# Weight loads moved to ScalarE's queue, gates ahead of transposes and queries, and a third buffer for the window tables of a one-core hybrid block

## The chip, the cores and the metric

The kernel runs on one core of a Trainium2 chip. The time is the device time of one execution in microseconds (us). The engines are PE (TensorE, matmuls), DVE (VectorE), ACT (ScalarE), POOL (GpSimd) and SP (SyncE, which only starts transfers). A DMA is started by an instruction on the queue of an engine (here of SP, ACT or POOL), and every engine works through its instructions strictly in the order that was fixed when the program was built.

## The reference, cut to what matters

Two layers over 512 latent and 256 context tokens, width 1024. Layer 0 is multi-head latent attention with 16 heads, layer 1 a bidirectional S5 state-space layer with a GLU; the weights are modulated by `c`.

```python
for i in range(DEPTH):                       # 0: attention, 1: S5
    sh, sc, gt = jnp.split(cond @ w_mod[i] + b_mod[i], 3, axis=-1)
    h_lat = x * (1.0 + sc[:, None]) + sh[:, None]
    y_lat, y_ctx = _mla_mixer(...) if kind == 0 else _s5_mixer(...)
    x = _layernorm(DEEPNORM_ALPHA * x + gt[:, None] * y_lat, ln_g[i], ln_b[i])
# layer 0
q_dn, kv_dn, k_rope, gate = jnp.split(h @ w_in, MLA_SPLITS, axis=-1)   # gate: 16 heads x 128
q_abs = jnp.einsum('bnhd,chd->bnhc', q[..., :MLA_NOPE], w_uk)
p = jax.nn.softmax(s_all * scale)            # 768 keys
v = jnp.einsum('bnhc,chv->bnhv', o_lat, w_uv); y = (v * silu(gate)) @ w_out
# layer 1: per group of 16 channels, 64 complex states
lam_bar = jnp.exp(lam * dt); powers = jnp.exp(lam_dt * arange(1, 129))
xs = scan of lam_bar * x + b_bar @ u; y = real(xs @ cmat)
```

## The kernel before, in words

Every product in full precision is three matmuls of split operands: `split` writes a high part on ACT (a cast, L65) and a low part `source - high` on DVE or, where it is asked for, on POOL (also L65). A projection is then `mm<-hh,whi`, `mm<-hl,whi`, `mm<-hh,wlo` (L81 to L83).

A scheduler fixes each engine's order at build time from the order of the code and its own estimate, so an edit moves instructions far from its own line. All transfers that SP's and ACT's queues start share eight semaphores in turn, so an issue can also have to wait for the transfer that had its semaphore before.

The stages, by the profile's times:

- 0 to 72 us: the input, the first modulation (L574), and the first projections of layer 0 (queries, keys, rotary part).
- 72 to 349 us, the **gate stage**: 16 gates, one for each head (`gate(m)`), each 48 matmuls, a tanh on ACT (L698) and a multiply on DVE (L699). The products of layer 1's and layer 0's remaining modulation run between them (`mod_steps`; a *step* is one 768 KB load of `w_mod` into a tile `pair`, L98, and the matmuls `modps<-pair` of L103). In the same stage POOL computes the parameters of S5 (`s5_params`: complex products `cmul`, L237 to L242, on 128x128 tiles that lie in the memory of `Qh`, `Ql`, `Vh`, `Vl`, `K`, `Ch`, whose proper contents come afterwards), PE transposes the coefficients (`s5_coefs`, L301), which leave as `pind`, and POOL and PE make the tables of S5 in 32 *chunks* of 4 groups: POOL writes `wo` and `bk` (L345 to L361), PE multiplies them (the *lag product*, `mm<-wo,bk`, L365 and L368), and the result `ks` is stored as `kd`. 20 chunks stand in the gate stage, 12 in attention.
- 349 to 806 us, **attention**: 80 *units* (5 for each head): scores (L793 to L797), softmax on DVE and ACT (L807 to L813), transposes, values, and the product with `w_uv`, for which the weight `absw` is loaded and split to `uh`, `ul` (L508, L65). The rotary and nope weights `uqr` are loaded (L468) and split to `whi`, `wlo` two heads at a time. After chunk 31 POOL makes 32 *window tables* (`win_early`): `pind` is loaded into a tile `wo` (L385), `Bc` into a half of `pw` (L386), six POOL instructions multiply them in place (L390 to L395), and SP stores the tile as `wid` (L404). There are two tiles `wo` and two halves of `pw`.
- 806 to 1774 us: output projection, layer norm, S5, GLU, output. PE's order is the same there in both kernels.

In the code of before SP starts all of these loads and stores, and POOL does the low parts of `uqr` and `absw` (`split(..., pool)`). The tiles that hold the first weights of modulation take turns: 4 `G`, 7 `M`, 2 `pair`.

Of the kernel before, what the change touches and what calls it, by code (L numbers as in the profile page):

```python
# [18 lines left out]
P = 128  # L19
# [5 lines left out]
HEADS = 16  # L25
# [6 lines left out]
def hybrid_mla_s5(ctx, tc, I, O):  # L32
# [13 lines left out]
    KEPT = 4  # L46
# [42 lines left out]
    def mod_steps(layer, c0, n, wt, ps, work, i):  # L89
# [35 lines left out]
    def mod_gt(layer, rows, work, pieces):  # L125

        gtrow[layer] = dram.tile([2, D], F32, name=f"gtd{layer}")
        for j, a, b, c0 in pieces:
# [3 lines left out]
            sp.dma_start(out=br[q, a:b], in_=I["bgt"][layer, c].unsqueeze(0).broadcast_to([2, b - a]))  # L132
            dve.tensor_add(br[q, a:b], br[q, a:b], rows[q, a:b])
            sp.dma_start(out=gtrow[layer][:, c], in_=br[q, a:b])
# [14 lines left out]
    GR, NCH, S5IN = 128, 32, 20  # L149
# [6 lines left out]
    def s5_params(take, pw, cci):  # L156

        def slots(k):
# [28 lines left out]
        T1, T2, keep = slots(6), slots(6), slots(6)  # L187
# [86 lines left out]
        cps = [slots(6) for _ in range(3)]  # L274
# [16 lines left out]
        for l in range(5):  # L291
            pool.tensor_scalar_mul(lt[l][:, 2, :], lt[l][:, 1, :], -1.0)
            sp.dma_start(out=lamd[:, l], in_=lt[l])
        return cps

    def s5_coefs(cps, mm, tile):

        for k, cp in enumerate(cps):
# [6 lines left out]
            sp.dma_start(out=pind[7 - k, :, :, 0:64], in_=st[:, :, 0:64])  # L305
            sp.dma_start(out=pind[k, :, :, 64:128], in_=st[:, :, 64:128])

    cbs, made, whole = {}, [], []

    def s5_stores():  # L310
# [6 lines left out]
        while made:  # L317
            c, wo, ks = made.pop()
            sp.dma_start(out=wod[c], in_=wo)
            for q in range(4):  # L320
                g = 4 * (c % 4) + q
                sp.dma_start(out=kd[c // 4][g, :, 112:240], in_=ks[32 * q:32 * q + 16, :])
                sp.dma_start(out=kd[c // 4][g, :, 0:112], in_=ks[32 * q + 16:32 * q + 32, 0:112])
            if c % 4 == 3:
                whole.append(c // 4)

    def s5_chunk(work, mm, c, pw, cci, bks, dcol, eyek, end):
# [9 lines left out]
        s5_stores()  # L337
        cb = cbs.pop(c)
        wo = work.tile([P, 4, 2, P], F32, name="wo", bufs=2)
        t1 = work.tile([P, 4, 8, 16], F32, name="wt1", bufs=1)  # L340
        t2 = work.tile([P, 4, 8, 16], F32, name="wt2", bufs=1)
# [3 lines left out]
        pool.tensor_tensor(t1, cr, pr, op=ALU.mult)  # L345
        pool.tensor_tensor(t2, ci, pi, op=ALU.mult)
        pool.tensor_tensor(wr, t1, t2, op=ALU.subtract)
        pool.tensor_tensor(t1, cr, pi, op=ALU.mult)
        pool.tensor_tensor(t2, ci, pr, op=ALU.mult)
        pool.tensor_tensor(wi, t1, t2, op=ALU.add)  # L350
# [23 lines left out]
        if c == end:  # L374
            s5_stores()
            s5_stores()
# [38 lines left out]
    with ExitStack() as ctx_:  # L415
# [8 lines left out]
        cci = s5c.tile([P, 3, GR], F32, name="cci")  # L424
        bks = [s5c.tile([P, 4, 2, 48], F32, name=f"bk{i}") for i in range(2)]
# [1081 lines left out]
```

## Time and profile before

| | |
|---|---|
| median of three runs | 1778.39 us (1774.8 to 1779.83) |
| profiled execution, its time | 1775.6 us |
| its span, first to last instruction | 1773.8 us |
| mean granted TensorE clock | 0.941 of full speed |
| busy: PE, DVE, ACT, POOL | 1573.9, 948.8, 731.1, 657.7 us |
| first score matmul of attention | 349.2 us |
| POOL's last window table ends | 803.2 us |

"Busy" adds up the spans of instructions on one engine. A matmul takes longer when the granted clock is low, so a busy PE can still be a slow one; the column PEclk says what was granted. Idle time of an engine is put down to what ended it.

### The profile page before, as it was taken

The page shows a single profiled execution, that of the slowest core. Times are in us where ns is not written, and L with a number is a line of the kernel's source. Part 1 is how long each engine was busy: PE and PEld are TensorE (multiplying, and loading weights), DVE is VectorE, ACT ScalarE, POOL GpSimd, SP SyncE. Part 2 cuts the span into 40 slices and gives each one's busy share as a digit, 9 for nine tenths or more (in the row PEclk, how much of TensorE's full clock was granted, in tenths as well). Part 3 has the DMA queues.
Part 4 walks back from the last instruction along what each step waited for, and adds up shares of the span by engine and source line. Part 5 has one row for each costly group of instructions (what it writes and reads, how often), then busy time and mean ns, then how long its engine had stood idle before and what let it go on. Part 6 is the DMA issues. An engine that isn't in the chain of part 4 may idle for free.

```text
span 1773.8 us, 26950 instructions
## 1 busy us (share of the span) xinstructions
PE 1573.9 (89%) x9870; PEld 1313.6 (74%) x9870; DVE 948.8 (53%) x2478; ACT 731.1 (41%) x1253; POOL 657.7 (37%) x705
## 2 busy tenths in 40 slices
PE   7548788999887977789999999999869999999997
PEld 4435467887786867678887999988658888888876
DVE  7352222376565755667435288899953433333336
ACT  2221122365545644556214666767473222222220
POOL 2999758899677878771000000000000000000022
PEclk9868798999989988989999999999889999999999
DMA  9216776564455565555424866578462333333442
GB/s 338 75 50 217 240 238 194 161 208 121 143 176 163 169 166 166 164 166 172 125 77 134 258 214 230 171 270 320 154 243 77 123 109 108 108 107 107 128 156 72
DMA packets 157132, 293.60 MB, mean 166 GB/s; under 512 B 55068, under 2 KB 86856, under 8 KB 155976
## 3 DMA queue, kind: packets, MB, share of 16 engines
q1 hardware_dynamic: 122056, 279.07, 48.6%
q10 hardware_dynamic: 34880, 12.78, 2.8%
q8 instruction: 78, 1.28, 0.3%
q14 instruction: 54, 0.44, 0.1%
q0 software_dynamic: 64, 0.03, 0.0%
HBM read 230.39 MB, written 69.55 MB: 169 GB/s over the span
## 4 chain that ended last, share of the span: by engine, by line
PE 53%; DMA 18%; POOL 16%; DVE 5%; issue 4%; ACT 3%; SPq 0%; ACTq 0%; POOLq 0%
PE mm L81 15%; PE mm L83 15%; PE mm L82 15%; DMA wo<-pind 8%; DMA wid<-wo 4%; PE mm L1134 3%; DMA pair<-in_w_mod_dram 2%; DMA wraw<-in_wout_dram 2%; POOL wo L395 1%; POOL pw L393 1%; PE mm L1268 1%; POOL wt L391 1%; POOL bk L361 1%; POOL wo L394 1%; POOL wt L390 1%
## 5 line engine op out<-in xcount | busy, mean ns | idle before, releaser
L65 DVE TENSOR_TENSOR wlo<-wraw,whi 128x1024 fp32r<-128x1024 f32 (+1 forms) x155 | 178.5, 1153 | 337.0 <-ACT whi L65 332.7
L1371 POOL TENSOR_TENSOR x<-x,row_g 128x1024 f32<-128x1024 f32 x4 | 11.3, 2846 | 926.0 <-DMA wraw<-in_wout_dram 886.6
L65 ACT CAST whi<-wraw 128x1024 fp32r<-128x1024 f32 (+1 forms) x155 | 149.4, 965 | 401.3 <-PE mm L82 268.2
L81 PE MATMUL mm<-st,whi 128*128 128x512 f32 x512 | 204.2, 399 | 5.2 <-ACT st L76 5.1
L83 PE MATMUL mm<-st,wlo 128*128 128x512 f32 x512 | 202.5, 396 | 0.0
L82 PE MATMUL mm<-st,whi 128*128 128x512 f32 x512 | 201.4, 393 | 0.8 <-DVE st L77 0.8
L81 PE MATMUL mm<-h,whi 128*128 128x512 f32 (+1 forms) x384 | 138.7, 362 | 0.2 <-DVE bnmv L917 0.2
L82 PE MATMUL mm<-h,whi 128*128 128x512 f32 (+1 forms) x384 | 137.1, 358 | 0.8 <-DVE h L1077 0.8
L83 PE MATMUL mm<-h,wlo 128*128 128x512 f32 (+1 forms) x384 | 136.5, 356 | 0.0
L81 PEld LDWEIGHTS mm<-st,whi 128*128 128x128 f32 x512 | 97.5, 190 | 26.8 <-ACT st L76 6.3
L81 PE MATMUL mm<-hh,whi 128*128 128x512 f32 (+1 forms) x320 | 112.2, 361 | 3.2 <-DVE hh L599 3.2
L82 PEld LDWEIGHTS mm<-st,whi 128*128 128x128 f32 x512 | 97.3, 190 | 23.3 <-DVE st L77 1.6
L83 PEld LDWEIGHTS mm<-st,wlo 128*128 128x128 f32 x512 | 97.4, 190 | 22.6
L83 PE MATMUL mm<-hh,wlo 128*128 128x512 f32 (+1 forms) x320 | 109.7, 346 | 1.1 <-DVE wlo L65 1.0
L82 PE MATMUL mm<-hl,whi 128*128 128x512 f32 (+1 forms) x320 | 110.4, 347 | 0.0
L65 DVE TENSOR_TENSOR ptl<-tr,pth 128x384 fp32r<-128x384 f32 (+1 forms) x160 | 79.0, 524 | 17.3 <-ACT pth L65 16.5
L65 ACT CAST pth<-tr 128x384 fp32r<-128x384 f32 (+1 forms) x160 | 68.5, 462 | 45.9 <-PE tr L832 45.3
L808 ACT ACTIVATE p<-sc,mx 128x768 f32<-128x768 f32 (+1 forms) x96 | 73.6, 766 | 27.9 <-DVE mx L807 27.6
L807 DVE TENSOR_REDUCE mx<-sc 128x1 f32<-128x768 f32 (+1 forms) x96 | 73.8, 772 | 17.4 <-PE sc L797 16.4
L81 PEld LDWEIGHTS mm<-h,whi 128*128 128x128 f32 x384 | 72.9, 190 | 12.0 <-issue 0.5
L82 PEld LDWEIGHTS mm<-h,whi 128*128 128x128 f32 x384 | 73.0, 190 | 10.8 <-DVE h L1077 1.1
L83 PEld LDWEIGHTS mm<-h,wlo 128*128 128x128 f32 x384 | 72.9, 190 | 10.4
(371 smaller groups left out, 4196.5 us busy)
## 6 DMA issues: line engine op xcount, KB each, us to landing
wraw<-in_wglu_dram SPq DMA_DIRECT2D x64, 512.0 KB
wraw<-in_win_dram SPq DMA_DIRECT2D x52, 512.0 KB
wod<-wo SPq DMA_DIRECT2D x32, 512.0 KB
wo<-pind SPq DMA_DIRECT2D x32, 512.0 KB
pw<-in_Bc_dram SPq DMA_DIRECT2D x32, 512.0 KB
wid<-wo SPq DMA_DIRECT2D x32, 512.0 KB
pt<-wid SPq DMA_DIRECT2D x32, 512.0 KB
wo<-wod SPq DMA_DIRECT2D x32, 512.0 KB
```

The source lines that it names most:

```text
L65: return act.copy(hi, src).ins, (eng or dve).tensor_tensor(lo, src, f(hi), op=ALU.subtract).ins
L81: pe.matmul(ps, lh, rh, start=first, stop=False)
L82: pe.matmul(ps, lh, rl, start=False, stop=False)
L83: pe.matmul(ps, ll, rh, start=False, stop=last)
L361: pool.tensor_tensor(bk[rows, :, :, 16 * d:16 * d + 16], b1[rows], b2[rows], op=ALU.add)
L390: eng.tensor_tensor(t1, pr, br, op=ALU.mult)
L391: eng.tensor_tensor(t2, pi, bi, op=ALU.mult)
L393: eng.tensor_tensor(bi, pr, bi, op=ALU.mult)
L394: eng.tensor_tensor(pr, t1, t2, op=ALU.add)
L807: dve.reduce_max(mx[:, 1:2], s, axis=AX.X, negate=True)
L808: act.activation(p[:, a:b], s, AF.Exp, bias=mx[:, 1:2], scale=1.0, accum_out=mx[:, 2:3])
L1134: pe.matmul(o[:, r, 96 * q:96 * (q + 1)], wi[:, q, r, :], us[m][:, 4 * (c % 2) + q, :], start=True, stop=True)
```

## The change

Seven things change together.

1. The loads of `w_mod`, of the gates' weights (`wraw`, L69), of `uqr` and `absw`, the stores of spilled gates and their return, and the coefficients' stores `pind` are started by ACT's queue. The stores `lamd` are started by POOL's. SP keeps the traffic of the tables.
2. The lag product of chunk c is emitted with chunk c+1 (`late`). `wo` has three buffers in the gate stage, two afterwards.
3. `s5_coefs` and `queries` (the casts of `qd` to `Qh`, `Ql`) are emitted after gate 1. S5's parameters lie in the tiles of `G` and in a new tile `ext`, which also holds `cci` and the two `bk`, instead of in `K`, `Ch`, `Vh` and `Vl`.
4. No modulation step is emitted before gate 2 (`if m >= 2`).
5. The first weights of modulation lie in `hh`, `hl`, `M` and one `pair`. Gates 0 to 11 are spilled to DRAM instead of 4 to 15, and three of them are called back before attention begins.
6. The low parts of `uqr` and `absw` are made by DVE.
7. The window tables take three tiles in turn (`ext` and two `wo`).

```diff
     def split(hi, lo, src, eng=None):
         return act.copy(hi, src).ins, (eng or dve).tensor_tensor(lo, src, f(hi), op=ALU.subtract).ins
 
-    def wsplit(wp, src, n=1024):
+    def wsplit(wp, src, n=1024, q=sp):
         raw = wp.tile([P, n], F32, name="wraw", bufs=2)
-        sp.dma_start(out=raw, in_=src)
+        q.dma_start(out=raw, in_=src)
...
         def load(kc):
             loaded[kc] = wt()[:, :4 * n]
-            sp.dma_start(out=loaded[kc], in_=I["w_mod"][layer, kc * P:(kc + 1) * P, c0:c0 + 4 * n])
+            act.dma_start(out=loaded[kc], in_=I["w_mod"][layer, kc * P:(kc + 1) * P, c0:c0 + 4 * n])
...
-    GR, NCH, S5IN = 128, 32, 20
+    GR, NCH, S5IN, WO = 128, 32, 20, [3]
...
-        cps = [slots(6) for _ in range(3)]
+        cps = [slots(6, take2) for _ in range(3)]
...
-            sp.dma_start(out=lamd[:, l], in_=lt[l])
+            pool.dma_start(out=lamd[:, l], in_=lt[l])
...
-            sp.dma_start(out=pind[7 - k, :, :, 0:64], in_=st[:, :, 0:64])
-            sp.dma_start(out=pind[k, :, :, 64:128], in_=st[:, :, 64:128])
-
-    cbs, made, whole = {}, [], []
-
-    def s5_stores():
+            act.dma_start(out=pind[7 - k, :, :, 0:64], in_=st[:, :, 0:64])
+            act.dma_start(out=pind[k, :, :, 64:128], in_=st[:, :, 64:128])
...
+    def s5_lags(work, mm, c, wo, bk, dcol, eyek):
+
+        sp.dma_start(out=wod[c], in_=wo)
+        s5_lay()
...
-        made.append((c, wo, ks))
+        for q in range(4):
+            g = 4 * (c % 4) + q
+            sp.dma_start(out=kd[c // 4][g, :, 112:240], in_=ks[32 * q:32 * q + 16, :])
+            sp.dma_start(out=kd[c // 4][g, :, 0:112], in_=ks[32 * q + 16:32 * q + 32, 0:112])
+        if c % 4 == 3:
+            whole.append(c // 4)
...
+        wo = work.tile([P, 4, 2, P], F32, name="wo", bufs=WO[0])
...
+        late.append(lambda: s5_lags(work, mm, c, wo, bk, dcol, eyek))
+        while len(late) > (c < end):
+            late.pop(0)()
...
-        cci = s5c.tile([P, 3, GR], F32, name="cci")
-        bks = [s5c.tile([P, 4, 2, 48], F32, name=f"bk{i}") for i in range(2)]
+        ext = s5c.tile([P, 9 * GR], F32, name="ext")
+        cci = ext[:, 0:3 * GR].rearrange("p (r g) -> p r g", g=GR)
+        bks = [ext[:, 3 * GR * i:3 * GR * i + 3 * GR].rearrange("p (q r x) -> p q r x", r=2, x=48) for i in (1, 2)]
...
-                sp.dma_start(out=raw, in_=I["uqr"][hp])
+                act.dma_start(out=raw, in_=I["uqr"][hp])
                 st["w"] = lw[0]("whi"), lw[0]("wlo")
-                split(*st["w"], raw, pool)
+                split(*st["w"], raw)
...
-                sp.dma_start(out=wa, in_=I["absw"][h])
+                act.dma_start(out=wa, in_=I["absw"][h])
                 st["u"] = ls.tile([P, P], F32R, name="uh", bufs=1), ls.tile([P, P], F32R, name="ul", bufs=1)
-                split(*st["u"], wa[:, 384:512], pool)
+                split(*st["u"], wa[:, 384:512])
...
-            wtile = itertools.cycle(["G"] * KEPT + ["M"] * 7 + ["pair"] * 2)
+            wtile = iter(["hh", "hl"] * KC + ["M"] * 7 + ["pair"])
...
-                    wg.append(wsplit(wp, I["win0"][4 + len(G) + len(wg)]))
+                    wg.append(wsplit(wp, I["win0"][4 + len(G) + len(wg)], q=act))
...
+                G.append(gv.tile([P, T], F32, name="G") if m >= HEADS - KEPT else gsp.tile([P, T], F32, name="Gs"))
...
+            def queries():
+                for i in range(2):
+                    Qh.append(qkv.tile([P, T], F32R, name=f"Qh{i}"))
+                    Ql.append(qkv.tile([P, T], F32R, name=f"Ql{i}"))
+                    dve.tensor_copy(Qh[i], qd[i])
+                    dve.tensor_sub(Ql[i], qd[i], f(Qh[i]))
...
+                    if m >= 2:
+                        mod_more()
+                if m >= 2:
                     mod_more()
-                mod_more()
+                if m == 1:
+                    s5_coefs(cps, mm, t512)
+                    queries()
                 for fn in prep0.pop(m, ()):
                     fn()
-                tables(3 if m == 0 else 1 + (m in (5, 10)))
+                tables(2 if m == 0 else 1 + (m % 4 == 2))
...
-                sp.dma_start(out=G[h], in_=Gd[h])
+                act.dma_start(out=G[h], in_=Gd[h])
+        for h in range(AHEAD):
+            gate_back(h)
...
+            WO[0] = 2
...
+                    pts = itertools.cycle([(s5c, "ext", [P, 9 * GR], 1)] + [(work, "wo", [P, 4, 2, P], 2)] * 2)
                 if LAST < i < len(units) - 1 and i % 3 != 0:
-                    win_early(lambda: (work.tile([P, 4, 2, P], F32, name="wo", bufs=2), btp[:, len(early) % 2]),
-                              lambda: [work.tile([P, 4, P], F32, name=f"wt{k}", bufs=1) for k in (1, 2)], [pool],
-                              i < len(units) - 7)
+                    def tabs():
+                        where, name, shape, bufs = next(pts)
+                        pt = where.tile(shape, F32, name=name, bufs=bufs)
+                        if name == "ext":
+                            pt = pt[:, 0:8 * GR].rearrange("p (g r x) -> p g r x", r=2, x=P)
+                        return pt, btp[:, len(early) % 2]
+                    win_early(tabs, lambda: [work.tile([P, 4, P], F32, name=f"wt{k}", bufs=1) for k in (1, 2)],
+                              [pool], i < len(units) - 7)
```

Three places of the order that come of it. First **PE after the projections**. Before, the 14 transposes of the coefficients (`mm<-ident,K` and `mm<-ident,Ch`) begin there, and gate 0 (`mm<-hh,whi` of 512 columns) comes behind them:

```order
L83 MATMUL mm<-hh,wlo 128x256
L301 MATMUL mm<-ident,K_271 128x128 x4
L301 MATMUL mm<-ident,K_272 128x128 x6
L301 MATMUL mm<-ident,Ch 128x128 x3
L652 MATMUL mm<-t_962,ones 128x512
L652 MATMUL mm<-t_962,ones 128x256
L81 MATMUL mm<-hh,whi 128x512
```

Now gate 0 follows the projections, and at its end, ahead of gate 1, stand eight whole modulation steps (32 matmuls in a row) and the lag product of chunk 0, which reads `bk` in `ext`:

```order
L83 MATMUL mm<-hh,wlo 128x256
L103 MATMUL modps<-pair,sT 2x384 x32
L325 MATMUL mm<-wo,ext 32x128 x8
L328 MATMUL mm<-wo,ext 32x16 x8
L81 MATMUL mm<-hh,whi 128x512
```

The transposes have moved behind gate 1, and the steps, which lay one at a time between the matmuls of several gates, have closed up into one row.

Second **ACT at the same place** (before, SP started these loads, with stores of tables between them). The tanh of gate 1 is the `Gs<-mm` of 512 columns at the end:

```order
L710 ACTIVATE Gs<-mm 128x256
L69 DMA wraw<-in_win_dram 128x1024
L700 DMA gd_1115<-Gs 128x768
L98 DMA pair<-in_w_mod_dram 128x1536 x8
L108 COPY modrow_985<-modps 2x384 x4
L98 DMA pair<-in_w_mod_dram 128x1536 x2
L331 COPY ks<-mm 128x112
L710 ACTIVATE Gs<-mm 128x512
```

All eight loads have one tile `pair` to go to, so that each is started when PE has done with the one before.

Third **SP in the window tables** (the number behind a tile's name is its instance). Before:

```order
L385 DMA wo_5405<-pind_81 128x1x1024
L404 DMA wid2_5470<-wo_5254 128x1024
L386 DMA pw_5029<-in_Bc_dram 128x1x1024
L385 DMA wo_5472<-pind_81 128x1x1024
L404 DMA wid3_5598<-wo_5405 128x1024
L386 DMA pw_5029<-in_Bc_dram 128x1x1024
L508 DMA wmod_5719<-in_absw_dram 128x512
```

and now:

```order
L405 DMA wid0_5223<-ext_5064 128x1024
L387 DMA pw_5000<-in_Bc_dram 128x1x1024
L386 DMA ext_5376<-pind_81 128x1x1024
L405 DMA wid1_5374<-wo_5178 128x1024
L387 DMA pw_5000<-in_Bc_dram 128x1x1024
L386 DMA wo_5443<-pind_81 128x1x1024
L405 DMA wid2_5441<-wo_5225 128x1024
L387 DMA pw_5000<-in_Bc_dram 128x1x1024
L386 DMA wo_5571<-pind_81 128x1x1024
L405 DMA wid3_5569<-ext_5376 128x1024
```

The load of `pind` still stands behind the store that frees its tile. Before, `wo_5472`, loaded behind the store of table 2, is table 4: while it loads, one other table is on hand. Now `ext_5376`, loaded behind the store of table 0, is table 3: two others are on hand. The load of `absw` has left SP's row.

## Rows read from the trace of the kernel before

**Rows 1.** Window: us, busy of PE, PEld, DVE, ACT, POOL; PE clock, DMA share, GB/s.

```profile
150.00:200.00 50.00, 30.98 (x254) 19.20 (x252) 16.42 (x29) 7.47 (x16) 42.42 (x53) 0.75 0.78 245
```

**Rows 2.** Waits of PE, 50 to 150 us: total, times, longest.

```profile
PE mm L301 <- POOL Ch L239: 12.9, 2, 6.8
PE mm L301 <- POOL K L239: 11.2, 3, 6.2
```

**Rows 3.** Waits of PE, 150 to 349 us.

```profile
PE modps L103 <- DMA pair<-in_w_mod_dram: 24.2, 10, 5.7
```

**Rows 4.** Timeline of DVE, multiplies of gates 0, 4 and 15 (first halves).

```profile
116.83 0.69 DVE L699 SCALAR_TENSOR_TENSOR G<-G,mm 128x512 f32<-128x512 f32 x1 [0.77 <-ACT G L698]
...
207.32 0.69 DVE L699 SCALAR_TENSOR_TENSOR Gs<-Gs,mm 128x512 f32<-128x512 f32 x1 [6.58 <-ACT Gs L698]
...
346.05 0.69 DVE L699 SCALAR_TENSOR_TENSOR Gs<-Gs,mm 128x512 f32<-128x512 f32 x1 [5.68 <-ACT Gs L698]
```

**Rows 5.** Chain of waits, 60 to 350 us: start, us, what.

```profile
170.86 6.28 DMA pair<-in_w_mod_dram
177.18 1.50 PE modps L103 x8
...
191.86 6.72 DMA pair<-in_w_mod_dram
```

**Rows 6.** Timeline of POOL: last complex product, two chunks' starts, last window table.

```profile
179.29 0.45 POOL L242 TENSOR_TENSOR Ql<-Ql,Vh 128x128 f32<-128x128 f32 x1
...
363.26 1.11 POOL L345 TENSOR_TENSOR wt<-cb,pw 128x512 f32<-128x512 f32 x1
...
372.44 1.11 POOL L345 TENSOR_TENSOR wt<-cb,pw 128x512 f32<-128x512 f32 x1
...
801.85 1.30 POOL L395 TENSOR_TENSOR wo<-pw 128x512 f32<-128x512 f32 x1
```

**Rows 7.** Timeline of PE, first score matmul of attention.

```profile
349.18 0.50 PE L793 MATMUL sc<-Ch,pair 128*128 128x512 f32 x1 [0.24 <-DVE Gs L699]
```

**Rows 8.** Waits of PE, 349 to 810 us.

```profile
PE mm L83 <- POOL ul L65: 44.0, 6, 11.0
PE sc L793 <- ACT pair L65: 7.6, 1, 7.6
```

**Rows 9.** Busy time by window, attention; columns as in rows 1.

```profile
525.00:550.00 25.00, 25.00 (x176) 22.68 (x175) 20.51 (x41) 17.70 (x42) 20.49 (x17) 1.00 0.59 162
...
625.00:650.00 25.00, 15.09 (x86) 13.48 (x85) 11.29 (x20) 6.24 (x15) 20.16 (x18) 0.80 0.58 157
```

**Rows 10.** POOL's instructions by line and form, 350 to 806 us.

```profile
L392 POOL TENSOR_TENSOR pw<-wo,pw 128x512 f32<-128x512 f32 x32 | 42.1, 1315 | 0.0
...
L65 POOL TENSOR_TENSOR wlo<-modrow,whi 128x512 fp32r<-128x512 f32 x7 | 9.7, 1379 | 0.2 <-ACT whi L65 0.2
L65 POOL TENSOR_TENSOR ul<-wmod,uh 128x128 fp32r<-128x128 f32 x15 | 6.9, 459 | 0.0
```

**Rows 11.** Chain of waits, 590 to 640 us.

```profile
600.65 4.67 DMA wid<-wo
...
605.33 6.38 DMA wo<-pind
...
634.45 9.54 DMA wo<-pind
```

**Rows 12.** Timeline of DVE and of POOL, 60 to 64 us.

```profile
63.18 1.28 DVE L65 TENSOR_TENSOR wlo<-wraw,whi 128x1024 fp32r<-128x1024 f32 x1 [5.14 <-ACT whi L65]
...
62.93 0.46 POOL L239 TENSOR_TENSOR K<-Ql,Vh 128x128 f32<-128x128 f32 x1
63.46 1.32 POOL L240 TENSOR_TENSOR Ql<-Vh 128x128 f32<-128x128 f32 x1
```

**Rows 13.** Waits of SP's queue, 350 to 806 us.

```profile
SPq L385 <- DMA wid<-wo: 82.5, 30, 5.5
SPq L508 <- POOL ul L65: 16.9, 7, 3.9
```

More of the change, by code (lines that the diff above doesn't have):

```diff
@@ L316, in s5_stores @@
                 sp.dma_start(out=toed[k][16 * i:16 * i + 16], in_=src[:, :, 16 * (7 - i):16 * (7 - i) + P])
[L317 to L325, printed above, removed]
@@ L372, in s5_chunk, with load @@
         dve.scalar_tensor_tensor(ks[:, 0:16], eyek, dcol[:, c:c + 1], o[:, 0:16], op0=ALU.mult, op1=ALU.add)
-        made.append((c, wo, ks))
+        for q in range(4):
[4 more added lines that the diff above has]
+            whole.append(c // 4)
+    def s5_chunk(work, mm, c, pw, cci, bks, dcol, eyek, end):
+        def load(c):
+            cbs[c] = work.tile([P, 4, 2, 32], F32, name="cb", bufs=2)
+            sp.dma_start(out=cbs[c], in_=I["CB"][:, 4 * c:4 * c + 4])
+        gs = slice(4 * c, 4 * c + 4)
+        if c not in cbs:
+            load(c)
+        if c < end:
+            load(c + 1)
+        cb = cbs.pop(c)
+        wo = work.tile([P, 4, 2, P], F32, name="wo", bufs=WO[0])
+        t = work.tile([P, 4, 8, 16], F32, name="wt1", bufs=1)
+        cr, ci = (cb[:, :, r, 0:16].unsqueeze(2).broadcast_to([P, 4, 8, 16]) for r in range(2))
+        pr, pi = (pw[:, r, :, gs].rearrange("p j g -> p g j").unsqueeze(3).broadcast_to([P, 4, 8, 16]) for r in range(2))
+        wr, wi = (wo[:, :, r, :].rearrange("p g (j c) -> p g j c", c=16) for r in range(2))
+        pool.tensor_tensor(wr, cr, pr, op=ALU.mult)
+        pool.tensor_tensor(t, ci, pi, op=ALU.mult)
+        pool.tensor_tensor(wr, wr, t, op=ALU.subtract)
+        pool.tensor_tensor(wi, cr, pi, op=ALU.mult)
+        pool.tensor_tensor(t, ci, pr, op=ALU.mult)
+        pool.tensor_tensor(wi, wi, t, op=ALU.add)
+        b1 = work.tile([P, 4, 2, 16], F32, name="b1", bufs=1)
+        b2 = work.tile([P, 4, 2, 16], F32, name="b2", bufs=1)
+        bb = cb[:, :, :, 16:32]
+        pool.tensor_tensor(b1, bb, cci[:, 0:2, gs].rearrange("p r g -> p g r").unsqueeze(3).broadcast_to([P, 4, 2, 16]),
+                           op=ALU.mult)
+        pool.tensor_tensor(b2, bb[:, :, ::-1, :], cci[:, 2, gs].unsqueeze(2).unsqueeze(3).broadcast_to([P, 4, 2, 16]),
+                           op=ALU.mult)
+        bk = bks[c % 2]
+        for d, rows in enumerate((lo_, up_)):
+            pool.tensor_tensor(bk[rows, :, :, 16 * d:16 * d + 16], b1[rows], b2[rows], op=ALU.add)
+        late.append(lambda: s5_lags(work, mm, c, wo, bk, dcol, eyek))
+        while len(late) > (c < end):
+            late.pop(0)()
@@ L374, in s5_chunk @@
         if c == end:
-            s5_stores()
-            s5_stores()
+            s5_lay()
     wid = {}
@@ L564, in mod_part @@
                         n = next(wtile)
-                        w = pair() if n == "pair" else (gv if n == "G" else gm).tile([P, T], F32, name=n)
+                        w = pair() if n == "pair" else (gm if n == "M" else hp).tile([P, T], F32, name=n)
                         w = w[:, :256 * (k1 - k0)].rearrange("p (k c) -> p k c", c=256)
@@ L617, in proj, with place @@
                 return out
-            names = iter(("Qh0", "Qh1", "Ql0", "Ql1", "Vh", "Vl", "K1", "K2", "Ch", "Cl"))
-            cps = s5_params(lambda: qkv.tile([P, T], F32, name=next(names)), pw, cci)
+            names = iter(("Qh0", "Qh1", "Ql0", "Ql1", "G"))
+            def place():
+                n = next(names)
+                return (gv if n == "G" else qkv).tile([P, T], F32, name=n)
+            cps = s5_params(place, lambda: gv.tile([P, T], F32, name="G"),
+                            ext[:, 3 * GR:].rearrange("p (s g) -> p s g", g=GR), pw, cci)
             for bk in bks:
@@ L681, in hybrid_mla_s5 @@
             Vl = qkv.tile([P, NT, P], F32R, name="Vl")
-            Qh = [qkv.tile([P, T], F32R, name=f"Qh{i}") for i in range(2)]
-            Ql = [qkv.tile([P, T], F32R, name=f"Ql{i}") for i in range(2)]
             wg = []
```

70 lines of the change are left out of this document (21 added, 49 removed).

## Prediction

> **What bounds the kernel now.** I read the windows first, because the shares of the whole span hide that the stages differ: PE is busy 89% of the span, but in the gate stage a window of 50 us holds 31 us of matmuls at three quarters of the clock [rows 1]. PE waits there, and what it waits for is told by its waits: before 150 us the transposes of the coefficients stand in its queue and wait for POOL's parameters, 12.9 and 11.2 us [rows 2]; after that it waits for loads of `w_mod`, 24.2 us in ten pieces [rows 3]. Gate 0's first multiply comes out at 116.8 us, gate 4's at 207.3, gate 15's at 346.1 [rows 4], the first score at 349.2 [rows 7]: the first four gates are slow, the last eleven take 12.6 us each ((346.05 - 207.32) / 11).
>
> In attention (349.2 to about 806 us: the last window table ends at 803.15 [rows 6], PE's last unit just after) PE could go faster. A window such as 525 to 550 us is full of matmuls at full clock; 625 to 650 has 15.1 us at 0.80 [rows 9]. The wait behind it is for `ul`, 44.0 us in six pieces, and 7.6 us for `pair` [rows 8]. `ul` is 0.46 us of POOL's work [rows 10], so 11 us of waiting are not its price: it stands in POOL's queue behind the instructions of a window table, and these wait for a load. The chain of waits there is store of `wid` (4.67 us), load of `pind` into the same tile (6.38, once 9.54), POOL, and again [rows 11]. So POOL's window tables, bound by two tiles, drive SP, POOL and through `ul` PE.
>
> **The change part by part: the gate stage.** With the transposes behind gate 1, gate 0 no longer waits for POOL: 116.8 less 24.1 is 92.7 us for its first half [rows 2, 4]. The transposes' own matmuls and their smaller waits go too, and the second half follows; as an estimate these two cancel, and gate 0 ends near 92.
>
> What now stands before gate 1 is new: eight modulation steps in a row, each loaded by ACT into one tile, so that a load begins when the step before has read it. The trace has this pattern by chance: load 6.28, step 1.50 at low clock, and three rounds later the load that begins at 191.86, so 7.0 us a round ((191.86 - 170.86) / 3) [rows 5]. Eight rounds are 56 us: 92 to 148. ACT's queue holds nothing urgent behind the loads but gate 1's tanh, which waits for PE anyway.
>
> Behind the steps PE needs POOL's `bk` for chunk 0, which lies in `ext` and so comes after POOL's whole parameter chain. That chain ends at 179.3 us now [rows 6], with eight whole chunks inside it; a chunk is 9.2 us (372.44 - 363.26) [rows 6]. In the new order three chunks stand inside, without their `bk`, about 7 us each: 179.3 - 73 + 21 = 127, and some 10 us for `bk`, the clearing of two tiles and five transfers that POOL now starts: about 137. This hides behind the 148 of the loads, by 11 us only.
>
> From there 14 more gates at 12.6 us are 176; this pitch already has in it the steps, lag products and waits of the last eleven gates of before. I add 6 us for the first half of gate 1 (half a pitch), as estimates 5 for the coefficients' transposes that have come here and 4 because PE comes out of 56 us of waits at low clock, and 3 from the last multiply to the first score [rows 4, 7]: 148 + 6 + 176 + 5 + 4 + 3 = 342. Before it was 349.2, so this stage gives 7 us. The bounds: 320 when weights on ACT's queue remove the remaining waits for `w_mod` too (a part of rows 3), 362 when a load takes 9.5 us, as the slowest in rows 11, instead of 5.5 (eight times 2.5 us a round more).
>
> **The change part by part: attention.** POOL first has chunks 20 to 31, 12 x 9.2 = 110 us, and 3 us pass before the first: 113. Then come 32 window tables of six instructions, 6 x 1.31 = 7.9 us [rows 10]. A tile's round is make 7.9, store 4.7, load 6.4 and the issues, 19.2 us and more with the slow loads: with two tiles 9.6 to 11 us a table, and the trace has (803.15 - 463) / 32 = 10.6, from the sum's own start. With three tiles the same round gives 6.4 to 7.1, less than POOL's 7.9: POOL becomes the bound of the tables, at 7.9 us, and I take 8.0.
>
> `ul` and `wlo` leave POOL (6.9 + 9.7 = 16.6 us [rows 10]) and go to DVE. What they cost on DVE is bounded by DVE's own split of 1024 columns, 1.28 us [rows 12]: 128 and 512 columns are at most that, scaled about 0.2 and 0.65, so some 8 us on an engine that has 20.5 of 25 us even in its fullest window [rows 9]. PE's 44.0 us of waits for `ul` fall away; what is late next is the window table itself, because the loads on ACT's queue share their semaphores with the tables' transfers: in the new order the issues of unit 69 wait for a transfer of table 29. So attention can't outrun the tables: 113 + 30 x 8.0 = 353 us to unit 69, then ten units. PE alone needs for 80 units 456.8 - 51.6 = 405 us without the two waits [rows 8], and about 380 when the clock also stays up (625 to 650 loses a fifth of 15 us [rows 9]; I take eight windows as like it): 4.7 to 5.1 a unit, 47 for ten. In all 400 us, where PE alone would end at 380 to 405. Attention ends at 342 + 400 = 742 instead of 806.
>
> **A rule against it.** The splits moved to DVE read two operands in SBUF, and rows 12 show what this does to POOL: its instruction that began under DVE's split of 1.28 us took 1.32 us, not 0.46. So POOL is held up by no more than the 8 us of the moved splits, against the 16.6 us that it gets rid of, and the sum keeps its sign; of the 0.1 us a table that I added this is the reason. The Trainium skill goes further, on the page SBUF — State Buffer, section "SBUF: two separate sides": DVE and GpSimd share a port pair that is locked for a whole instruction, and whoever comes second "fully blocks". The first half of that the trace shows (0.46 to 1.32). The other half, DVE blocked by POOL, no row here shows for attention; by it 24 splits would each wait for the rest of a table's instruction of 1.31 us [rows 10], 0.65 on average, 16 us if all of it were on the path, and the time 1729 instead of 1713.
>
> **The sum.** 349.2 - 342 = 7, and 456.8 - 400 = 57; PE's order after attention is unchanged, so nothing else is to move: -64. The profiled execution's own time is 1775.6 us (2.8 under the median of the runs, 1778.4). 1775.6 - 64 = 1711.6, and against the median 1714. I say 1713.
>
> **Rivals.**
>
> *Transfers stay the bound.* Tables made a third faster move a third more: DMA engines are at 0.58 to 0.59 busy with tables at 10.6 us [rows 9], so 0.77 at 8.0, about what 150 to 200 us has (0.78, 245 GB/s [rows 1]). A store of 5.5 and loads of 9.5 [rows 11, 13] make a round of 23, 7.7 a table; with `Bc` and SP's in-order queue in the way perhaps 9.3: attention 113 + 279 + 47 = 439, end 781, time 1753.
>
> *PE is the bound.* The tables finish early, ACT's issues never wait, the clock stays at 1.0: attention 380, gate stage ending at 328: 708, time 1680. Against it: the order ties units to tables.
>
> *No gain.* The pace of the tables stays at 10.1 or more, since the round is set by transfers that only share the same machines: 342 + 113 + 30 x 10.1 + 47 = 805, time 1778, the same. The Trainium skill speaks for this on the page DMA: Bandwidth & Descriptors, section "Issuing engines are not separate DMA queues": transfers from several queues run on the same 16 engines, and only issue time is saved. By that rule alone moving loads from SP to ACT buys nothing. Against it as a whole: the third tile does not ask for bandwidth but for overlap, and 0.59 leaves room.
>
> *Slower.* ACT's queue is where the softmax and the high parts run, in order. Some 34 loads (15 `absw`, 7 `uqr`, 12 gates) stand in it now, and each can wait for a buffer or a semaphore. SP waited 2.4 us on average at `absw` (16.9 in 7, longest 3.9) [rows 13], which harmed nobody. If each of the 34 holds ACT for 2.4 us, that is 82 us more on the softmax: 1713 + 82 = 1795. It decides from 1.9 us each. Against it: what SP waited for was POOL's `ul`, which DVE now makes at once.
>
> **How the numbers follow.** Chances: forecast 0.54 (own range 1690 to 1736), transfers stay the bound 0.21, PE the bound 0.12, no gain 0.06, slower 0.07. The range leaves out the last two, the upper third of the second and a part of the fast end: 1678 to 1764. Less than 0.3% (5 us) this kernel's runs can't tell from no change. Faster 0.88, same 0.05, slower 0.07.
>
> **What would show it.** In the changed kernel: gate 0's second multiply near 92 us and no wait of PE for POOL at the transposes; eight loads `pair` with PE waiting 5 us before each, some 40 to 45 in all; gate 1's multiply near 154; the first score at 335 to 350. In attention no wait for `ul`; window tables at 7.8 to 8.3 us from start to start; POOL over 90% busy there; the last table at about 700. It is wrong if PE's wait for `bk` or `ext` ends well after 150 us (then POOL's chain, not the loads, sets gate 1), if POOL still waits for `wo<-pind` or now for `pw<-in_Bc`, or if ACT's queue shows waits for transfers in attention with PE idle behind them.

## The result, and the profile after

The changed kernel takes 1750.65 us (median of four runs, 1748.03 to 1752.73) against 1778.89 in the same series: ratio 0.984, interval 0.982 to 0.987. That is 28 us faster; 65 were forecast (1713). The time lies in the stated range, but well under half of the forecast gain came. The profiled execution took 1748.03 us, its span is 1746.0 us, and its mean granted clock 0.948.

Three places of the profile tell where the gain is and where it is not. First the gate stage, by window as in [rows 1]:

```profile
100.00:150.00 50.00, 10.22 (x56) 0.77 (x56) 8.03 (x9) 0.00 (x0) 48.94 (x74) 0.50 0.59 189
150.00:200.00 50.00, 44.55 (x390) 36.45 (x391) 10.56 (x16) 12.21 (x35) 38.16 (x46) 0.93 0.61 192
```

and the chain of waits through the first of these windows, start, length, what:

```profile
100.77 1.14 DVE Cl L737
101.93 5.33 DMA pair<-in_w_mod_dram
107.40 1.50 PE modps L103 x8
...
146.84 5.12 DMA pair<-in_w_mod_dram
152.01 1.46 PE modps L103 x8
153.46 0.85 PE mm L325 x16
```

PE is busy for 10 of 50 us, and its granted clock falls to 0.50 of full speed, the lower of its two levels (1.2 of 2.4 GHz). The eight loads run one behind the other as forecast, in 6.4 us a round ((153.47 - 101.93) / 8), but they begin at 101.9, not at 92: the tile `pair` still holds `ckv` (the keys and values before their split), which DVE reads for the last time to make `Cl`. PE's waits from 50 to 150 us, in place of [rows 2]; from 150 to 363 us; and before from 150 to 349 us:

```profile
PE modps L103 <- DMA pair<-in_w_mod_dram: 41.3, 7, 12.1
...
PE mm L325 <- POOL wo L358: 12.3, 4, 5.0
PE mm L325 <- POOL wo L361: 11.6, 4, 5.1
...
PE mm L365 <- POOL wo L347: 4.0, 2, 3.0
PE mm L365 <- POOL wo L350: 1.6, 2, 1.3
```

Gate 1's first multiply (DVE) and the first score (PE), which answer to [rows 4, 7]:

```profile
162.16 0.69 DVE L712 SCALAR_TENSOR_TENSOR Gs<-Gs,mm 128x512 f32<-128x512 f32 x1 [6.17 <-ACT Gs L710]
...
362.86 0.40 PE L819 MATMUL sc<-Ch,pair 128*128 128x512 f32 x1
```

Attention begins 13.7 us later than before, not 7 earlier. Second the window tables, POOL's timeline (first and last; [rows 6]), and POOL's waits from 60 to 800 us. Behind them, in the same order, the first table of before and its waits from 60 to 810 us:

```profile
498.69 1.26 POOL L391 TENSOR_TENSOR wt<-ext,pw 128x512 f32<-128x512 f32 x1 [17.56 <-DMA kd<-ks]
...
774.70 1.31 POOL L396 TENSOR_TENSOR wo<-pw 128x512 f32<-128x512 f32 x1
```

```profile
POOL wo L356 <- DMA cb<-in_CB_dram: 33.1, 8, 9.9
POOL wt L391 <- DMA kd<-ks: 17.6, 1, 17.6
POOL wt L391 <- DMA pw<-in_Bc_dram: 14.6, 14, 4.2
```

```profile
474.33 1.30 POOL L390 TENSOR_TENSOR wt<-wo,pw 128x512 f32<-128x512 f32 x1 [8.69 <-DMA kd<-ks]
...
POOL wt L390 <- DMA wo<-pind: 62.7, 23, 5.5
```

Before, table 0 began at 474.3 and the last ended at 803.15: 10.28 us each. Now 498.7 to 776.0: 8.67 each. The 62.7 us of waits for `pind` [rows 11] have become 14.6 us for `Bc`. So the tables start 24.4 us later and run 51.5 us shorter, and their end is 27.1 us earlier. Attention's last multiply (DVE, before and after) is 26.9 us earlier, and the span 27.8, so the gain is made by the end of attention:

```profile
808.98 0.42 DVE L850 TENSOR_TENSOR G<-mm,G 128x256 f32<-128x256 f32 x1 [0.38 <-PE mm L83]
...
782.03 0.42 DVE L876 TENSOR_TENSOR G<-mm,G 128x256 f32<-128x256 f32 x1 [0.38 <-PE mm L83]
```

Third the waits of PE in attention (345 to 800 us), which answer to [rows 8]:

```profile
PE sc L819 <- ACT pair L65: 9.6, 5, 6.1
PE mm L325 <- POOL wo L361: 9.0, 3, 5.1
PE mm L81 <- DVE G L876: 7.9, 13, 0.8
PE sc L822 <- DVE xp L462: 6.7, 4, 3.2
```

The 44 us for `ul` are gone and nothing of that size is in their place. From the first score to the last multiply PE is busy for 375.7 of 419.2 us, and the rest are small waits that DVE, ACT and POOL end.

### The profile page after: what moved, and what is told of

It is laid out like the page before. It is cut to its first block, busy times and chain, and to the rows that moved or that the text cites. A ratio compares the mean times of both kernels' runs of the same rounds, so it can differ in the third digit from the quotient of the medians.

```text
span 1746.0 us, 26883 instructions
## 1 busy us (share of the span) xinstructions
PE 1560.3 (89%) x9870; PEld 1305.9 (75%) x9870; DVE 962.8 (55%) x2502; ACT 729.9 (42%) x1253; POOL 650.2 (37%) x686
## 4 chain that ended last, share of the span: by engine, by line
PE 57%; DMA 14%; DVE 12%; POOL 6%; ACT 5%; issue 3%; SPq 2%; ACTq 0%; DVEq 0%; POOLq 0%
PE mm L81 16%; PE mm L83 16%; PE mm L82 16%; PE mm L1167 3%; DMA pair<-in_w_mod_dram 3%; DMA wraw<-in_wout_dram 2%; DMA cb<-in_CB_dram 1%; DMA toed<-kd 1%; DMA pw<-in_Bc_dram 1%; PE tr L858 1%; DMA ext<-pind 1%; DVE wlo L65 1%; DMA wraw<-in_win_dram 1%; PE modps L103 1%; POOL wo L359 1%
## 5 line engine op out<-in xcount | busy, mean ns | idle before, releaser
L1404 POOL TENSOR_TENSOR x<-x,row_g 128x1024 f32<-128x1024 f32 x4 | 11.3, 2829 | 926.0 <-DMA x<-x1d 926.0
L65 DVE TENSOR_TENSOR ptl<-tr,pth 128x384 fp32r<-128x384 f32 (+1 forms) x160 | 79.1, 524 | 15.4 <-ACT pth L65 14.5
```

The costliest lines, as they stand in the source:

```text
L65: return act.copy(hi, src).ins, (eng or dve).tensor_tensor(lo, src, f(hi), op=ALU.subtract).ins
L1404: pool.tensor_tensor(x, x, rows["g0"], op=ALU.mult)
```

## The experiments

Each ratio is to the kernel before in the same series. "Table 0" is the start of the first window table and "last multiply" that of attention's last multiply in the profiled execution, in us. What was expected before each run is printed with it; it names two readings, theory A and rival B, and the times that each would give.

| kernel | median us | ratio, interval | table 0 | last multiply |
|---|---|---|---|---|
| before | 1778 | | 474.3 | 809.0 |
| the change | 1750.7 | 0.984 (0.982 to 0.987) | 498.7 | 782.0 |
| E1 loads behind the gates' tanh | 1759.1 | 0.988 (0.985 to 0.990) | 505.6 | 788.0 |
| E2 `cb` on POOL's queue | 1751.0 | 0.983 (0.981 to 0.986) | 506.2 | 784.4 |
| E4 before + third tile | 1742.2 | 0.978 (0.975 to 0.981) | 490.5 | 777.2 |
| E5 before + splits on DVE | 1794.5 | 1.008 (1.005 to 1.011) | 473.9 | 827.2 |
| E6 before + attention part | 1752.4 | 0.986 (0.983 to 0.989) | 484.9 | 782.0 |
| E7 gates 1 to 3 ahead | 1747.7 | 0.984 (0.981 to 0.987) | 496.6 | 777.7 |
| E8 change, wo tiles first | 1744.3 | 0.982 (0.979 to 0.986) | 499.5 | 779.1 |
| E9 = E7 + E8 | 1746.7 | 0.984 (0.979 to 0.989) | 496.3 | 784.0 |
| E10 short tables | 1792.6 | 1.010 (1.006 to 1.013) | 496.1 | 823.4 |
| E11 E4 + loads on ACT | 1740.0 | 0.979 (0.975 to 0.983) | 489.9 | 780.9 |
| E12 E4, wo tiles first | 1741.4 | 0.981 (0.977 to 0.985) | 475.9 | 770.8 |
| E13 gate part alone | 1781.8 | 1.003 (1.001 to 1.005) | 496.1 | 815.2 |
| E14 change, splits on POOL | 1761.2 | 0.991 (0.989 to 0.994) | 512.2 | 788.1 |
| E15 change, DVE splits twice | 1756.0 | 0.988 (0.987 to 0.990) | 499.8 | 788.5 |
| E16 E14, wo tiles first | 1748.9 | 0.984 (0.982 to 0.985) | 499.5 | 785.6 |
| E17 E9, splits on POOL | 1756.8 | 0.989 (0.987 to 0.991) | 499.0 | 785.4 |
| E18 gate part + third tile | 1742.7 | 0.980 (0.978 to 0.983) | 500.9 | 783.9 |
| E19 lag products at once | 1758.9 | 0.991 (0.989 to 0.993) | 510.4 | 795.5 |

**What holds gate 1: E1.** The loads are tied to the gates, so that the row of eight no longer stands ahead of gate 1.

```diff
-                    load()
+                    with tc.issue_after(last_t[0]):   # the tanh emitted last
+                        load()
```

> The changed kernel, with each load of w_mod queued on ACT behind the tanh that was emitted last, so that the eight loads no longer stand ahead of gate 1. Theory A (the eight loads in a row hold gate 1 back): gate 1's first multiply comes at 115 to 125 us instead of 162, the first score 25 to 35 us earlier than 363, the time about 1720. Rival B (POOL's parameter chain, which ends at 147 and which PE needs for chunk 0's lag product ahead of gate 1, would hold gate 1 at nearly the same time): gate 1's multiply at 155 to 160, the eight steps are now to be done later, first score within 10 us of 363, time 1740 to 1760.

Rival B. Waits of PE, 50 to 150 us:

```profile
PE mm L325 <- POOL ext L372: 55.0, 1, 55.0
```

With the loads gone PE waits as long for POOL's `bk`: two things end within 5 us of each other, and taking one away buys 4 us at gate 1 (158.25). The first score then comes 10 us later than in the change (373.0), and the time is 8 us longer.

**Why the later gates are slow: E2.** `cb`'s loads go to POOL's queue (`pool.dma_start` for `sp.dma_start`).

> The changed kernel, with the loads of cb started by POOL's queue instead of SP's. Theory A (the later gates take 14.2 us instead of 12.6 because cb stands in SP's row behind kd stores that wait for PE's lag product, now a piece later): POOL's waits for cb fall from 33 us to under 10, the pitch of gates 2 to 15 from 13.2 towards 12.3, first score 8 to 15 us before 363, time 1735 to 1742. Rival B (the pitch is PE's own: matmuls at a low granted clock and waits for w_mod): cb waits fall but the first score stays within 4 us of 363, time within 5 us of 1750.

POOL's waits for `cb` fall from 33.1 to 8.5 us and the first score is 6 us earlier (357.1), but the time is the same. Theory A holds for the waits and in part for the first score, rival B for the time.

**The parts of attention: E4, E5, E6, E11.** E4 puts the third tile alone into the kernel before (with `ext`, which takes in `cci` and `bk` as in the change), E5 the splits on DVE alone, E6 both with the loads of `absw` and `uqr` on ACT, E11 the third tile and these loads with the splits on POOL.

```diff
+                    pts = itertools.cycle([(s5c, "ext", [P, 9 * GR], 1)] + [(work, "wo", [P, 4, 2, P], 2)] * 2)   # E4, E6, E11
...
-                split(*st["u"], wa[:, 384:512], pool)
+                split(*st["u"], wa[:, 384:512])                   # E5, E6; w alike
...
-                sp.dma_start(out=wa, in_=I["absw"][h])
+                act.dma_start(out=wa, in_=I["absw"][h])           # E6, E11; uqr alike
```

> The kernel before, with only the third tile for the window tables added (ext and two wo in turn). Theory A (two tiles bound the tables, the tables bound PE through ul): tables at 8.0 to 8.8 us instead of 10.3, PE's wait for ul falls from 44 to under 20 us, attention 30 to 45 us shorter, time 1735 to 1750. Rival B (what counted was that ul stood in POOL's row): tables faster, but POOL now never idles, so ul still waits behind them, 30 to 45 us in all, and the time falls by under 15 us: 1764 to 1778.

> The kernel before, with only the splits of ul and wlo moved from POOL to DVE. Theory A (two tiles bound the tables): PE's wait for ul goes, tables stay near 10 us each and end near 800, PE runs ahead of them only as far as the order lets it; attention ends 0 to 15 us earlier, time 1763 to 1778. Rival B (ul in POOL's row was the cause): attention 35 to 50 us shorter, time 1730 to 1743.

Theory A in E4: 36 to 37 us come from the third tile alone, more than from the whole change, and the wait for `ul` shrinks by itself, though POOL still makes it. E5 went past both expectations, 15 us slower than before: `absw` then stands in SP's row behind stores that wait for tables (158.4 us of waits of SP, in 30 pieces). PE's waits, in E4 and then in E5:

```profile
PE mm L83 <- POOL ul L65: 11.6, 3, 7.8
```

```profile
PE mm L514 <- DMA wmod<-in_absw_dram: 54.4, 5, 14.7
```

> The kernel before with the attention part of the change alone: the third tile (ext first), the splits of ul and wlo on DVE, and the loads of absw and uqr on ACT's queue; its gate stage stays. Theory A (the gate stage of the change costs what it seems to cost, 14 us, and its attention part is worth 42): first score at 349 to 353, no wait of PE for ul or absw over 10 us, attention 412 to 420 us, time 1730 to 1740, under the 1742 of the third tile alone. Rival B (moving the loads and splits adds nothing to the third tile, since the tables end at the same time): attention 425 to 430 us, time 1740 to 1748.

> The kernel before with the third tile and with the loads of absw and uqr on ACT's queue; the splits stay on POOL. Theory A (the 10 us by which the attention part, 1752, is slower than the third tile alone, 1742, come from loads that hold up ACT's row): 1748 to 1756, with ACT waiting 8 us or more at a cast for a table's transfer. Rival B (they come from the splits on DVE, the fullest engine after PE): 1738 to 1745.

E6 comes out beyond both, slower than the third tile alone. E11 does not show the loads alone to be the reason (1740.0): with the gate stage of before, the 12 us come with the splits on DVE. What these do is not settled by it, for in E6 ACT also stands for 11.2 us in one piece at a cast, until a transfer of `kd`, where no wait of ACT for a transfer in E11 is over 6.6.

**Doubling and undoing the splits: E14, E15.** E14 gives them back to POOL in the changed kernel, E15 makes each low part twice on DVE.

> The changed kernel with one thing undone: the splits of ul and wlo are on POOL again. Theory A (the splits on DVE cost the 12 us by which the attention part with them, 1752, is slower than the third tile with loads on ACT and splits on POOL, 1740): 1734 to 1743. Rival B (POOL is now the bound, so 17 us of splits on it lengthen the tables): 1750 to 1765.

> The changed kernel with each low part of uqr and absw computed twice on DVE (24 instructions, some 8 us, more; the result is the same). Theory A (work or port conflicts of these splits on DVE are what costs): 1756 to 1764. Rival B (it is where they stand in DVE's row and what they wait for, not their work): within 4 us of the changed kernel, 1746 to 1755.

E15 is 5 us slower than the change, so the work costs, but by less than it is: the splits of attention take 38.2 us on DVE there instead of 18.3, and a quarter of the 19.9 us more reaches the time. And theory A falls in E14: with the change's gate stage and loads on ACT, splits on POOL are 10 us slower than splits on DVE. Rival B has the time but not the reason, for the tables run at 8.64 us each, as in the change; they begin 13.5 us later. ACT's timeline there shows what happens around table 0 (at 512.2):

```profile
497.30 0.23 ACT L834 ACTIVATION_READ_ACCUMULATOR p<-sc,mx 128x1 f32 x1
505.54 0.33 ACTq L510 DMA_DIRECT2D wmod<-in_absw_dram  x1
505.92 0.59 ACT L65 CAST pair<-mm 128x512 fp32r<-128x512 f32 x1 [8.39 <-DMA kd<-ks]
```

ACT stands for 8.0 us before it can start the load of `absw`, and the casts behind it stand too. This is the mechanism that the prediction gave to its slower rival; in the changed kernel it appears once with 7.3 us and twice with 7.5 in all, not 34 times. As the change has nearly the same wait, it does not explain the 10 us between the two.

**The gate stage: E13, E18, E7, E19.** E13 takes the attention part out of the change, E18 leaves only its third tile in. E7 puts gates 1 to 3 ahead of what POOL must deliver (`tables(0 if m < 3 else 1 + m % 2)`, steps from gate 1 on and tied to the tanh as in E1, `s5_coefs` and `queries` after gate 4). E19 emits each lag product with its own chunk (`while late:`).

> The changed kernel without its attention part: two tiles wo for the window tables, the splits of ul and wlo on POOL, loads of absw and uqr on SP. What is left is its gate stage, the later lag products and the return of the gates on ACT's queue. Theory A (a later first score is given back, because the units catch up with tables that start when chunk 31 is done): first score at 358 to 368, last multiply within 6 us of before's 809, time 1775 to 1787. Rival B (the gate stage's 14 us are lost): last multiply at 820 to 826, time 1790 to 1797.

> The gate stage of the change with the third tile, loads of absw and uqr on SP and splits on POOL: the counterpart of the third tile alone (1742) with the other gate stage. Theory A (the gate stage's later first score makes chunk 31 and with it table 0 later, and where the tables are near the bound the end moves with them): 1755 to 1766, table 0 at 498 to 512. Rival B (it is given back, as with two tiles, where it cost 3 to 5 us): 1742 to 1750.

> The changed kernel, with gates 1 to 3 and modulation steps between them ahead of the first lag product, and transposes and queries behind gate 4; the tables of the gate stage begin behind gate 3. Theory A (what gate 1 waits for from 92 to 153 us, the row of eight loads and POOL's chain together, is idle PE that gates could fill): PE busy 25 to 40 us more between 100 and 150 us, first score at 330 to 345 instead of 363, time 1715 to 1735. Rival B (POOL's chunks then set the pace, 17 of them from 147 us at 9.2 and more): PE waits for wo 20 us or more after 200 us, first score 350 to 362, time 1738 to 1752.

> The changed kernel with each lag product emitted with its own chunk instead of one piece later (wo keeps its three buffers in the gate stage). Theory A (the lag products a piece later do nothing for the gates but delay what hangs behind chunk 31): POOL's wait before table 0 falls under 12 us, time 1740 to 1747. Rival B (a piece later spares PE waits for wo in the gate stage): PE waits for wo over 30 us, first score later than 366, time 1751 to 1760.

In E13 the first score is 18.5 us later than before (367.7), and this costs 3 to 5 us with two tiles, as theory A had it. In E18 it is 13 us later than in E4 (366.1 and 353.1) and costs nothing with three: 1742.7 beside 1742.2, rival B. E7 does fill PE, 26.9 us busy from 100 to 150 us instead of 10.2, but the time stays within 3 us of the change: rival B, its first score is at 360, since PE then waits 47 us for POOL's `wo` and `bk` from 150 to 362 us (26.1, 14.0 and 7.2). E19 is 8 us slower than the change: the later lag products help, which the prediction had not priced at all. It has rival B's time but not its reason: PE waits only 11.3 us for `wo` before the first score, less than in the change (23.9). POOL's wait for `cb` before 350 us is 39.9 us (28.4 in the change), and table 0 is 11.7 us later.

**The start of the tables: E8, E12, and combinations: E9, E16, E17.** Tables in the order `wo`, `wo`, `ext`, in the change (E8), in E4 (E12), with E7's gates (E9), with splits on POOL (E16), with both (E17).

> The changed kernel, with the window tables taking wo, wo, ext in turn instead of ext, wo, wo, so that table 0 isn't loaded into the tile that chunk 31's bk still holds. Theory A (POOL's 17.6 us of waiting before table 0 comes from ext): that wait falls to 6 to 10 us, tables end 8 to 10 us earlier, time 1740 to 1745. Rival B (the wait is for Bc, whose tile pw POOL reads up to chunk 31, with pind and the stores all in flight at once): 15 to 20 us as now, time 1748 to 1753.

> The kernel before with the third tile, in the order wo, wo, ext. Theory A (table 0 waits for ext): POOL's wait before table 0 falls from 19.5 to about 14 us as it did in the changed kernel (17.6 to 14.1), time 1735 to 1742. Rival B (the start of the tables doesn't bound): time within 4 us of 1742.

> Both of the two edits before (gates 1 to 3 ahead of the first lag product; tables in the order wo, wo, ext). Theory A for both: the gains add, time 1707 to 1727. If only one holds, its gain alone. If the tables set the end of attention and start at the same time after chunk 31 whatever the gates do, an earlier first score is given back in attention: first score earlier by 20 us and more, but the last table within 5 us of 776.

> The changed kernel with the splits on POOL and the tables in the order wo, wo, ext. A candidate for a version better than both: if the two add (12 and 4 us) 1732 to 1740; if the start of the tables doesn't bound, as for the kernel before with the third tile (1741 against 1742), the same as with the splits alone.

> Gates 1 to 3 ahead of the first lag product, tables in the order wo, wo, ext, and the splits on POOL. The gates alone gave 3 us (1748), so 1728 to 1740 if the gains add; if an earlier first score is given back in attention, as it seems, the same as without them.

In E12 table 0 starts at 475.9, 15 us earlier than in E4, and the time is the same: rival B. In E8 the wait falls to 14.1 us only and the time by 6, at the edge of what the runs tell. E9, E16 and E17 all miss what their gains would add up to (1707 to 1727, 1732 to 1740, 1728 to 1740).

**Take the tables away: E10.** Four of the six POOL instructions of a table are left out, so the tables and what S5 makes of them are not the reference's.

> The changed kernel with four of the six POOL instructions of each window table left out (the tables, and so S5's output, are not the reference's). Theory A (at 363 to 782 us the pipeline of PE, DVE and ACT bounds attention, with POOL's tables just fast enough): tables end long before 776, the last unit's multiply still at 770 to 782, time 1738 to 1750. Rival B (the tables, through the transfers that ACT's issues wait for, bound the units): the last multiply at 725 to 755, time 1695 to 1725.

Both fell: 42 us slower. POOL's waits (350 to 820 us), and two windows, columns as in [rows 1]:

```profile
POOL wt L391 <- DMA pw<-in_Bc_dram: 123.8, 25, 16.5
```

```profile
525.00:550.00 25.00, 9.42 (x50) 8.04 (x49) 6.33 (x12) 4.03 (x10) 7.61 (x6) 0.76 0.62 207
...
750.00:775.00 25.00, 23.90 (x170) 21.68 (x169) 19.47 (x43) 17.71 (x42) 0.00 (x0) 1.00 0.05 12
```

Now the loads of `Bc`, for which there are two halves of `pw`, set 7.1 us a table ((724.2 - 496.1) / 32), and ACT waits for them: 21.3 us in two pieces at a cast `xp`. In the first of the two windows PE stands for over 15 of 25 us. The last table ends near 724, and what is left of attention then takes 99 us at 23.9 of 25 us of PE. With shorter POOL times the scheduler also laid the units out differently, so this run tells what the tables' transfers alone take, not what attention would be without the tables.

## Why the prediction was right and wrong

**Right: what bounded.** Two tiles bound the tables, the tables drove `ul`, and `ul` PE; E4 shows it with one edit. The pitch was forecast at 8.0 us and is 8.67 (14.6 us of waits for `Bc`, half a microsecond a table, and POOL's instructions a little longer than in [rows 10]: 8.0 us a table for six). PE's own work in attention was put at about 380 us and is 375.7.

**The step that failed first: the gate stage** ("148 + 6 + 176 + 5 + 4 + 3 = 342"). It is 362.9, 21 us more. Of this the "ends near 92" is 10 too early: PE is done with gate 0 at 95.3, and I looked at when gate 0 frees PE and not at when DVE frees the tile `pair`. The eight rounds were 4.5 us shorter than thought (51.5 for 56), and the first half of gate 1 took 8.7 us, not 6. From gate 1's multiply to the first score it is 200.7 us where the sum had 188: the pitch of the last eleven gates of before doesn't carry over. PE waits 23.9 us for POOL's `wo` there, where it waited 5.6 before, and the clock of the windows is 0.89 to 0.93. E2, which takes most of POOL's waits for `cb` away, gets 6 us back; the rest is not taken apart. That the chain of POOL's parameters "hides behind the 148 of the loads, by 11 us only" was right in kind: its first `bk` is done at 149.1, 4 us before the loads' last matmuls end at 153.5.

**The second: attention** ("113 + 30 x 8.0 = 353 us to unit 69, then ten units"). The 113 us are 118, and behind them stands a wait that the sum lacks: 17.6 us before table 0. The trace of before already has such a wait, 8.7 us; the prediction's 10.6 us a table counts it into the pace, which was 10.28. The 30 tables at 8.67 are 20 us more than at 8.0. Against that only 23 us follow on the thirtieth table, not 47. So 5 + 18 + 20 - 24 = 19 in attention, and with 21 from the gate stage these are the 40 us between the sum's 742 and 782.0. This follows the sum's own path. That the tables still pace attention, as "attention can't outrun the tables" has it, is not shown. In the changed kernel the last multiply follows the end of the last table by 6 us, as it did before. In E6 and E12 the last table ends at 758.2, and the last multiply follows by 24 and 13 us.

**What the sum took for additive isn't.** The first score came 21 us later than forecast, but E13 and E18 show that a later first score costs 0 to 5 us, and E7 that filling PE's idle window gives 3. So the gate stage explains little of the missing gain, and the step that cost it is the second: attention with three tiles does not come down to 400 us. Conversely the moved splits and loads, booked as a gain, cost 8 to 10 us on top of the third tile (E18 to the change, E4 to E6). By medians, added in this order, the change is the third tile (-36), the gate stage (0), and splits on DVE with loads on ACT (+8). The two moves have no fixed price either. With the gate stage of before, the loads on ACT cost nothing (E4 to E11, -2) and the splits on DVE 12 (E11 to E6). With the change's it is the other way round: the loads cost 18 (E18 to E14), and the splits on DVE gain 10 (E14 to the change), 5 (E16 to E8, within what the runs can tell) and 10 (E17 to E9).

**The rule that was weighed.** The prediction priced the splits on DVE at 0.2 and 0.65 us, and the other half of the rule (DVE blocked by POOL) at up to 16 us more that no row showed. Now rows show it. The 15 `ul` on DVE (first column minimum, median and maximum in ns), and one of them beside POOL's instruction of that moment:

```profile
L65 DVE TENSOR_TENSOR ul<-wmod,uh x15: 280/1084/1425, 405.2 to 772.3; 128x128 fp32r<-128x128 f32 x15
```

```profile
574.35 1.43 DVE L65 TENSOR_TENSOR ul<-wmod,uh 128x128 fp32r<-128x128 f32 x1
...
574.34 1.30 POOL L393 TENSOR_TENSOR pw<-wo,pw 128x512 f32<-128x512 f32 x1
```

A split that needs 0.28 us (at 492.4, while POOL waits) and begins under POOL's instruction ends behind it. Over 22 splits of attention DVE spends 18.3 us (12.2 for `ul`, 6.1 for `wlo`), where 8 were taken. The Trainium skill's page SBUF — State Buffer, section "SBUF: two separate sides", says just this of the port pair that DVE and GpSimd share: whoever comes second "fully blocks". The trace agrees in both directions. So the first of the two prices was 10 us too low for DVE's time. That this is why the change falls short is not shown: in E15 a quarter of the added split time reached the kernel's time, and next to the change the splits on POOL are slower.

**The rivals.** "Transfers stay the bound" gave 1753 with 9.3 us a table; the time is near by luck: the tables run at 8.67, 17.6 us pass before the first of them, and less follows on the last. "Slower" by ACT's row showed in single waits of 7 to 8 us, not as a pace. "No gain" fell with the third tile, but moving loads to ACT alone indeed gave nothing that the runs can tell (E11 beside E4). "PE is the bound" did not come: 43 us of small waits are left in attention. Of the signs, the last table was to end at about 700 and ends at 776.0, and POOL was not to wait for `pw<-in_Bc` and does so for 14.6 us.

**Open.** The 419 us that attention takes (362.9 to 782.0) aren't brought down to one cause. With three tiles and whatever start it is 411 to 429 us in E8, E18, E4 and E6. POOL's, ACT's and DVE's rows all reach PE by waits of under 10 us, and the interplay of gate stage, loads on ACT and splits (E14 21 us over E11, the change 2 us under E6) was measured, not explained; an edit also makes the scheduler lay out the units anew, which no run here separates.

The fastest kernels are E11, E12, E4 and E18, 1740 to 1743 us. They have the third tile and no splits on DVE. The third tile alone, with the rest left as it was (E4, E12), beats the change by about 9 us.

## What to carry to other kernels

Look for the buffer whose round (make, store, load) sets a pace; a third tile there was worth more than all moves of queues and engines around it. Before adding up stages, ask who is waiting for what at the seam: here 13 and 18.5 us at the seam were worth 0 to 5 us at the end. A moved load must be followed to its tile's last reader as well as to its queue. A split that reads two operands in SBUF took longer here on whichever of DVE and POOL found the other at work, and only a run tells how much of that reaches the time.

## What the runs showed of the hardware that was not expected

A DVE split of 128x128 took 0.28 us alone and up to 1.43 us beside POOL's 1.30 us instructions; at the first projections of before it was the other way round, 1.32 us for a POOL instruction of 0.46 [rows 12]. In these rows it went by who began first. The next split began 0.02 us ahead of POOL and took its 0.28 us, and POOL's instruction was the longer one:

```profile
626.28 0.28 DVE L65 TENSOR_TENSOR ul<-wmod,uh 128x128 fp32r<-128x128 f32 x1
...
626.30 1.41 POOL L393 TENSOR_TENSOR pw<-wo,pw 128x512 f32<-128x512 f32 x1
```

With POOL's work on a table cut to a third (E10), the two halves for `Bc` became the next round: two tables in 14.3 us, of which POOL takes 5.2 and a load of `Bc` mostly 10 to 11 (9.2 to 15.4 in the chain of waits), at a DMA share of 0.61 to 0.65 where the changed kernel's first 50 us show 0.87. A load that has room on the DMA engines can still be the bound, by the time that one of it takes.
